# A scan chunk's 64-column products in one run with the next chunk's B and C, and the skip as diagonal products on TensorE

## The chip, the cores and the metric

The kernel runs on one core of one Trainium2 chip. The metric is the device time of an execution in microseconds; three timed runs of the kernel before gave a median of 919.21 us (915.98 to 921.51).

## What is computed

The kernel is one layer of a diffusion block over 512 latent tokens with 256 context tokens before them: a mixer (a bidirectional Mamba-2 scan beside a grouped-query attention) and a hierarchical mixture of experts. The change is in the output of the scan. For each chunk of 128 tokens, each group g of 8 heads and each of the two directions the reference computes

```python
decay = jnp.where(lower, jnp.exp(jnp.where(lower, diff, 0.0)), 0.0)
cb = jnp.einsum('bcqgn,bcsgn->bcqsg', Cc, Bc)
y_diag = jnp.einsum('bcqsgr,bcsgrp->bcqgrp', cb[..., None] * decay, xdt)
y_off = jnp.einsum('bcqgn,bcgrpn,bcqgr->bcqgrp', Cc, h_in, jnp.exp(a_cs))
...
skip = p['d_skip'].astype(F32).reshape(SSD_GROUPS, SSD_HEADS_PER_GROUP)[..., None]
y = y_f + jnp.flip(y_b, axis=1) + xs.astype(F32) * skip
```

that is, for every head the product of a 128 x 128 mixing matrix with the chunk's tokens (128 x 64), the part that comes from the carried states, and the skip: the tokens times one number for each head.

## The kernel before

The program is written for a planner: every instruction has a priority, which counts up in the order of the code unless a `with rank(p)` sets it, and the planner fixes each engine's order by priority among what it believes ready at that time. Engines then run their lists in order.

The scan is `ssd(g)` (lines 540 to 630), called for the groups 0 and 1 (lines 717 and 721). It first carries the states through the chunks (`carry`, with weighted tokens in the two buffers `wx`), and then goes over four chunks c. For each chunk:

- lines 598 to 603: the products of B and C (two halves of 64 columns, tile `CT,BT` in the trace) into the PSUM buffer `s`, copied by ScalarE to `cb`
- line 605: GpSimd multiplies the tokens with the skip (`xs`)
- lines 606 to 612: the products of C with the carried states, `of` and `ob`, and VectorE's two multiplications out of PSUM into `y` and `y2`
- `mixing` (lines 579 to 594), for each half of the heads: factors are loaded from DRAM (line 585), masked by GpSimd (line 587), taken through the exponential by ScalarE (line 590), added and multiplied with `cb` by VectorE (lines 592 and 593): the mixing matrices M of four heads
- lines 616 to 620: for each head, and for each half of 64 rows of the output, a product of M and the tokens (tile `xl,M`, 64 columns); an fp32 product is two instructions, so there are 32 for a chunk
- lines 621 to 623: GpSimd adds `xs` to `y2`, VectorE adds `y2` and the product `yd` to `y`
- for group 0, `gated` (line 632) follows

The helper `mm` (line 107) issues all products, so they have this line in the trace. Beside the scan TensorE runs the projections: for group 0 those of `in_rows(0, z_sink)` and `scan_inputs(1)` (lines 715 and 718), for group 1 those of the queries (line 728). They have 128 columns and write the tile `a`; their weights are split into two parts by ScalarE (line 75) and by VectorE or GpSimd (line 76), and `scan_inputs` has a convolution on VectorE (lines 431 and 473). Both lists start at the same priority (`scanned[0]`, `scanned[1]`), so the two kinds of products are mixed on TensorE.

Of the kernel before, what the change touches and what calls it, by code (L numbers as in the profile page):

```python
# [8 lines left out]
F32 = mybir.dt.float32  # L9
# [3 lines left out]
AF = mybir.ActivationFunctionType  # L13
OP = mybir.AluOpType
# [79 lines left out]
def hybrid_block_kernel(ctx: ExitStack, tc: tile.TileContext, I, out):  # L94
    nc = tc.nc
    PE, V, S, G, SP = nc.tensor, nc.vector, nc.scalar, nc.gpsimd, nc.sync

    def pool(name, bufs=1, side="left", space=None, stack=None):
        kw = dict(name=name, bufs=bufs, reuse_waits="tile")
        if space is not None:  # L100
            kw["space"] = space
        else:
            kw["side"] = side
        return (stack or ctx).enter_context(tc.tile_pool(**kw))

    def mm(o, a, b, first, last):
        return PE.matmul(o, lhsT=a, rhs=b, start=first, stop=last)  # L107
# [6 lines left out]
    @contextmanager  # L114
    def rank(p):

        at, tc.cur_priority = tc.cur_priority, p
        yield
        tc.cur_priority = at
# [4 lines left out]
    def brow(ap, n):  # L124
        return bass.AP(tensor=ap.tensor, offset=ap.offset, ap=[[0, 128], [1, n]])
# [8 lines left out]
    def heads(ap, n):  # L134
        return ap.rearrange("p (h d) -> p h d", h=n)
# [11 lines left out]
    def pb(tag="b", dt=F32):  # L147
        return psb.tile([128, 512], dt, name=tag, bufs=tags.get(tag, 1))
# [8 lines left out]
    ident, tri_le, tri_ge = cst[:, 0:128], cst[:, 128:256], cst[:, 256:384]  # L157
# [165 lines left out]
    dsk = sdp.tile([128, 16], F32, name="dsk")  # L323
# [90 lines left out]
    grps = {0: {}, 1: {}}  # L414
# [124 lines left out]

    def ssd(g):  # L540

        r, ys = grps[g], {}
        lb, dec, wdt, ecs = dk["lb"], dk["dec"], dk["wdt"], dk["ecs"]
        gcol = slice(g * 512, (g + 1) * 512)

        def hs(d):
            return slice(d * 16 + g * 8, d * 16 + g * 8 + 8)

        def bc8(ap):
            return ap.to_broadcast([128, 8, 64])  # L550

        def weigh(t, d):
            wx = wk.tile([128, 512], F32, name="wx")
            x = r["xc"][:, t, :] if t < 2 else r["xl"][:, t - 2, :]
            V.tensor_tensor(heads(wx, 8), heads(x, 8), bc8(wdt[:, t, hs(d), None]), op=OP.mult)
            return wx

        def carry(o, h, t, d):

            wx = weigh(t, d)  # L560
            p = pb("s")
            mm(p, r["B"][:, t, :], wx, True, True)
            V.tensor_tensor(heads(o, 8), heads(h, 8), bc8(dec[:, t, hs(d), None]), op=OP.mult)
            V.tensor_add(o, o, p)

        hb, hf = (wk.tile([128, 4, 512], F32, name=n, bufs=1) for n in ("hb", "hf"))
        for d, o in ((1, hb[:, 3, :]), (0, hf[:, 0, :])):
            p = pb("s")
            for t in range(2):
                mm(p, r["B"][:, t, :], weigh(t, d), t == 0, t == 1)  # L570
            S.activation(o, p, AF.Copy)
        for i in range(3):
            carry(hb[:, 2 - i, :], hb[:, 3 - i, :], 5 - i, 1)
            carry(hf[:, i + 1, :], hf[:, i, :], 2 + i, 0)

        ng = wk.tile([128, 512], F32, name="ng", bufs=1)
        SP.dma_start(ng, brow(I["ssd_norm_g"][gcol], 512))

        def mixing(c, hh, cb):

            bc = wk.tile([128, 2, 4, 128], F32, name="bc", bufs=BC)
            for d, sg in ((0, 1), (1, -1)):
                h0 = d * 16 + g * 8 + 4 * hh
                s = csd[c, h0:h0 + 4, :]
                SP.dma_start(bc[:, d].rearrange("p h q -> p (h q)"),
                             bass.AP(tensor=s.tensor, offset=s.offset, ap=[[0, 128], [1, 512]]))
                G.affine_select(bc[:, d], bc[:, d], pattern=[[0, 4], [sg, 128]], compare_op=OP.is_ge,  # L587
                                fill=-1e30, base=0, channel_multiplier=-sg)
                for h in range(4):
                    S.activation(bc[:, d, h, :], bc[:, d, h, :], AF.Exp, bias=lb[:, c, h0 + h:h0 + h + 1])  # L590
            M = wk.tile([128, 4, 128], F32, name="M", bufs=MB)
            V.tensor_add(M, bc[:, 0], bc[:, 1])
            V.tensor_tensor(M, M, cb[:, None, :].to_broadcast([128, 4, 128]), op=OP.mult)
            return M

        for c in range(4):
            tk_ = slice(c * 128, (c + 1) * 128)
            p = pb("s")
            for a in range(2):
                o = slice(a * 64, a * 64 + 64)  # L600
                mm(p[o, 0:128], r["BT"][:, c * 128 + a * 64:c * 128 + a * 64 + 64], r["CT"][:, tk_], True, True)
            cb = wk.tile([128, 128], F32, name="cb")
            S.activation(cb, p[:, 0:128], AF.Copy)
            xs = wk.tile([128, 512], F32, name="xs", bufs=1)
            G.tensor_tensor(heads(xs, 8), heads(r["xl"][:, c, :], 8), bc8(dsk[:, g * 8:g * 8 + 8, None]), op=OP.mult)
            of, ob = pb(), pb()
            mm(of, r["CT"][:, tk_], hf[:, c, :], True, True)
            mm(ob, r["CT"][:, tk_], hb[:, c, :], True, True)
            y = wk.tile([128, 512], F32, name="y", bufs=4)
            y2 = wk.tile([128, 512], F32, name="y2", bufs=1)  # L610
            V.tensor_tensor(heads(y, 8), heads(of, 8), bc8(ecs[:, c, hs(0), None]), op=OP.mult)
            V.tensor_tensor(heads(y2, 8), heads(ob, 8), bc8(ecs[:, c, hs(1), None]), op=OP.mult)
            yd = pb()
            for hh in range(2):
                M = mixing(c, hh, cb)
                for h in range(4):
                    hc = slice((4 * hh + h) * 64, (4 * hh + h) * 64 + 64)
                    for a in range(2):
                        o = slice(a * 64, a * 64 + 64)
                        mm(yd[o, hc], M[:, h, o], r["xl"][:, c, hc], True, True)  # L620
            G.tensor_add(y2, y2, xs)
            V.tensor_add(y, y, y2)
            V.tensor_add(y, y, yd)
            ys[c] = y
            if g == 0:
                zt = wk.tile([128, 512], F32, name="zt", bufs=1)
                SP.dma_start(zt, z_d[c * 128:(c + 1) * 128, :])
                gated(y, zt, ng)
                SP.dma_start(y_d[c * 128:(c + 1) * 128, :], y)
        return ys, ng  # L630

    def gated(y, zt, ng):
        V.scalar_tensor_tensor(y, y, 0.5, zt, op0=OP.mult, op1=OP.mult)
        ss = wk.tile([128, 1], F32, name="ss")
        S.activation(wk.tile([128, 512], F32, name="y2", bufs=1), y, AF.Square, accum_out=ss)
        V.tensor_scalar(ss, ss, 1.0 / 512, 1e-6, op0=OP.mult, op1=OP.add)
        powc(ss, ss)
        V.scalar_tensor_tensor(y, y, ss, ng, op0=OP.mult, op1=OP.mult)
# [14 lines left out]
    def gate(o, p):  # L653
        S.activation(o, p, AF.Tanh, scale=0.5)
        V.scalar_tensor_tensor(o, o, 1.0, p, op0=OP.add, op1=OP.mult)
# [58 lines left out]
    wk = pool("wk", 2, side="right", stack=ssdst)  # L714
    in_rows(0, z_sink)
    with rank(scanned[0]):
        ssd(0)
    scan_inputs(1)
    scanned[1] = tc.cur_priority
    cvst.close()  # L720
    ys, ng = ssd(1)
    tc.cur_priority = scanned[1]
    eapst = ExitStack()
# [9 lines left out]
    def last_sink(t, hb_, p):  # L733
        zt = wk.tile([128, 4, 128], F32, name="M", bufs=MB).rearrange("p h q -> p (h q)")
        gate(zt, p)
        gated(ys[t], zt, ng)
# [14 lines left out]
    wrA, ca, cb = lt("wrA", 8, 20), lt("ca", 20), lt("cb", 20)  # L751
# [923 lines left out]
```

## Time and profile before

| | us |
|---|---|
| median of three runs | 919.21 |
| lowest and highest | 915.98, 921.51 |
| the profiled execution | 912.09 |
| its span in the profile | 909.8 |
| TensorE busy | 819.1 |
| VectorE busy | 696.8 |
| ScalarE busy | 420.2 |
| GpSimd busy | 319.8 |

The profile is of one execution; its times are counted from the start of the span. A busy TensorE is not TensorE at its peak: matmuls overlap, and a matmul that waits for the array counts as busy. In the rows PE is TensorE, DVE VectorE, ACT ScalarE and POOL GpSimd; a tile is written as out<-in.

### The profile page before, as it was taken

Reading aid. Unit: us, or ns where it says so; the run is one execution under the profiler, and the core shown is the slowest. Engines: PE = TensorE matmul, PEld = TensorE weight load, DVE = VectorE, ACT = ScalarE, POOL = GpSimd, SP = SyncE. Lnnn points to the kernel's source line nnn. Section 1 sums busy time; section 2 is a strip of 40 time slices with the busy share of each in tenths; the row PEclk is TensorE's granted clock in tenths of the full one; section 3 lists DMA queues with packets and bytes.
Section 4 is the critical chain, followed back from the end, with each engine's and each line's share of the span. In section 5 each row is a group of like instructions: output and inputs, shape, how many; then the busy total and the mean of one; then the engine's idle time right before and its main releaser. Section 6 shows DMA issues by size and latency. Waiting matters only on the chain. (4 is left out here: it accounts for less than half of the span.)

```text
span 909.8 us, 13605 instructions
## 1 busy us (share of the span) xinstructions
PE 819.1 (90%) x4974; PEld 569.0 (63%) x4974; DVE 696.8 (77%) x1074; ACT 420.2 (46%) x776; POOL 319.8 (35%) x230
## 2 busy tenths in 40 slices
PE   6999998899989999999988999899982799999992
PEld 2696676556776566776655656556652577777762
DVE  3575764886967897656776787877888999899977
ACT  2253443545563144453541444444433466776652
POOL 0012211426231273410059036540314555545524
PEclk9999999999999999999997999999996799999997
DMA  9966996436343133676053011120185999999974
GB/s 300 319 195 235 286 303 215 128 116 185 104 118 83 45 118 109 202 227 170 24 151 103 13 30 62 46 83 1 53 273 207 332 350 340 331 339 343 338 212 192
DMA packets 112349, 165.54 MB, mean 182 GB/s; under 512 B 13144, under 2 KB 78200, under 8 KB 112280
## 3 DMA queue, kind: packets, MB, share of 16 engines
q1 hardware_dynamic: 105560, 141.24, 48.8%
q0 software_dynamic: 6288, 21.84, 8.4%
q10 hardware_dynamic: 432, 1.57, 0.5%
q8 instruction: 39, 0.64, 0.3%
q14 instruction: 30, 0.25, 0.1%
HBM read 142.41 MB, written 22.21 MB: 181 GB/s over the span
## 5 line engine op out<-in xcount | busy, mean ns | idle before, releaser
L75 ACT ACTIVATE whi<-wraw 128x1024 fp32r<-128x1024 f32 (+1 forms) x100 | 104.1, 1045 | 74.7 <-PE a L107 40.8
L76 DVE TENSOR_TENSOR wlo<-wraw,whi 128x1024 fp32r<-128x1024 f32 (+1 forms) x73 | 94.7, 1303 | 24.0 <-ACT whi L75 23.3
L967 ACT ACTIVATE hxh<-b 128x512 f32<-128x512 f32 x96 | 55.7, 595 | 88.9 <-PE b L107 88.2
L76 POOL TENSOR_TENSOR wlo<-wraw,whi 128x1024 fp32r<-128x1024 f32 (+1 forms) x22 | 53.5, 2432 | 117.9 <-ACT whi L75 98.5
L943 DVE TENSOR_REDUCE mx<-s 128x1 f32<-128x768 f32 x64 | 61.0, 953 | 34.3 <-PE s L107 34.2
L473 DVE SCALAR_TENSOR_TENSOR acc<-u,cols,acc 128x770 f32<-128x770 f32 (+1 forms) x48 | 56.8, 1182 | 28.5 <-ACT acc L465 23.0
L107 PE MATMUL a<-whi,hxh 128*128 128x512 f32 (+2 forms) x176 | 70.7, 403 | 1.8 <-ACT hxh L263 1.8
L107 PE MATMUL a<-wlo,hxh 128*128 128x512 f32 (+2 forms) x176 | 69.8, 397 | 0.2 <-DVE wlo L76 0.2
L107 PE MATMUL a<-whi,hxl 128*128 128x512 f32 (+2 forms) x176 | 69.1, 394 | 0.0
L107 PE MATMUL a<-hxl,whi 128*128 128x512 f32 (+1 forms) x176 | 64.5, 367 | 0.0
L107 PE MATMUL a<-hxh,whi 128*128 128x512 f32 (+1 forms) x176 | 64.1, 364 | 0.0
L107 PE MATMUL a<-hxh,wlo 128*128 128x512 f32 (+1 forms) x176 | 63.9, 363 | 0.0
L590 ACT ACTIVATE bc<-bc,lb 128x128 f32<-128x128 f32 x128 | 40.6, 392 | 13.5 <-POOL bc L587 13.3
L107 PE MATMUL a<-whi,xh 128*128 128x512 f32 x102 | 43.8, 429 | 0.0
L1435 POOL DMA_INDIRECT acc<-y,rowi x15 | 26.5, 1768 | 48.5 <-DVE wlo L76 29.6
L107 PE MATMUL a<-wlo,xh 128*128 128x512 f32 x102 | 41.1, 402 | 0.1
L107 PE MATMUL a<-whi,xl 128*128 128x512 f32 x102 | 40.9, 401 | 0.0
L107 PEld LDWEIGHTS a<-whi,hxh 128*128 128x128 f32 x176 | 33.9, 193 | 10.9 <-issue 4.2
L107 PEld LDWEIGHTS a<-wlo,hxh 128*128 128x128 f32 x176 | 34.0, 193 | 9.7 <-issue 4.9
L107 PEld LDWEIGHTS a<-hxh,wlo 128*128 128x128 f32 x176 | 33.9, 193 | 9.2 <-issue 5.3
L107 PEld LDWEIGHTS a<-whi,hxl 128*128 128x128 f32 x176 | 33.7, 192 | 9.3 <-issue 4.6
L107 PEld LDWEIGHTS a<-hxl,whi 128*128 128x128 f32 x176 | 34.0, 193 | 7.4 <-issue 3.6
(489 smaller groups left out, 2169.4 us busy)
## 6 DMA issues: line engine op xcount, KB each, us to landing
wraw<-in_w_mod_dram SPq DMA_DIRECT2D x32, 512.0 KB
wraw<-in_w_in_dram SPq DMA_DIRECT2D x30, 512.0 KB
wraw<-in_w_down_dram SPq DMA_DIRECT2D x22, 512.0 KB
wraw<-in_w_gate_dram SPq DMA_DIRECT2D x40, 256.0 KB
wraw<-in_w_up_dram SPq DMA_DIRECT2D x40, 256.0 KB
mraw<-in_w_mod_dram SPq DMA_DIRECT2D x32, 256.0 KB
bc<-csd SPq DMA_DIRECT2D x32, 256.0 KB
wraw<-in_w_out_dram SPq DMA_DIRECT2D x8, 512.0 KB
```

The costliest lines, as they stand in the source:

```text
L75: self.nc.scalar.activation(hi, raw, AF.Copy)
L76: self.lo_engine(i).tensor_sub(lo, raw, hi.bitcast(F32))
L107: return PE.matmul(o, lhsT=a, rhs=b, start=first, stop=last)
L473: V.scalar_tensor_tensor(a, uk, wk_, a, op0=OP.mult, op1=OP.add)
L590: S.activation(bc[:, d, h, :], bc[:, d, h, :], AF.Exp, bias=lb[:, c, h0 + h:h0 + h + 1])
L943: V.tensor_reduce(mx[u][:, g:g + 1], pss_[:, 768 * i:768 * i + 768], axis=AX, op=OP.max)
L967: S.activation(PT[u][:, k], p, AF.Exp)
L1435: G.indirect_dma_start(out=acc, out_offset=bass.IndirectOffsetOnAxis(ap=rows, axis=0), in_=y, in_offset=None, compute_op=OP.add)
```

## The change

The skip becomes a product: for each head ScalarE makes a diagonal matrix (the identity times the head's number), kept in the two buffers `wx`, and TensorE adds the diagonal's product with the tokens to the product with M, in the same PSUM accumulation. GpSimd's multiplication and addition go. All products of a chunk are issued after both Ms are made, from the last head to the first, and are ranked at the priority that the scan began with; the products of B and C of the next chunk follow them there, so that they are no longer at the head of the chunk's loop.

```diff
--- before.py
+++ after.py
@@ -539,7 +539,7 @@
 
     def ssd(g):
 
-        r, ys = grps[g], {}
+        r, ys, first = grps[g], {}, tc.cur_priority
         lb, dec, wdt, ecs = dk["lb"], dk["dec"], dk["wdt"], dk["ecs"]
         gcol = slice(g * 512, (g + 1) * 512)
 
@@ -593,16 +593,22 @@
             V.tensor_tensor(M, M, cb[:, None, :].to_broadcast([128, 4, 128]), op=OP.mult)
             return M
 
-        for c in range(4):
-            tk_ = slice(c * 128, (c + 1) * 128)
+        def pairs(c):
+
             p = pb("s")
             for a in range(2):
                 o = slice(a * 64, a * 64 + 64)
-                mm(p[o, 0:128], r["BT"][:, c * 128 + a * 64:c * 128 + a * 64 + 64], r["CT"][:, tk_], True, True)
+                mm(p[o, 0:128], r["BT"][:, c * 128 + a * 64:c * 128 + a * 64 + 64], r["CT"][:, c * 128:c * 128 + 128], True, True)
+            return p[:, 0:128]
+
+        skip = [wk.tile([128, 4, 128], F32, name="wx") for _ in range(2)]
+        for h in range(8):
+            S.activation(skip[h // 4][:, h % 4], ident, AF.Copy, scale=dsk[:, g * 8 + h:g * 8 + h + 1])
+        p = pairs(0)
+        for c in range(4):
+            tk_ = slice(c * 128, (c + 1) * 128)
             cb = wk.tile([128, 128], F32, name="cb")
-            S.activation(cb, p[:, 0:128], AF.Copy)
-            xs = wk.tile([128, 512], F32, name="xs", bufs=1)
-            G.tensor_tensor(heads(xs, 8), heads(r["xl"][:, c, :], 8), bc8(dsk[:, g * 8:g * 8 + 8, None]), op=OP.mult)
+            S.activation(cb, p, AF.Copy)
             of, ob = pb(), pb()
             mm(of, r["CT"][:, tk_], hf[:, c, :], True, True)
             mm(ob, r["CT"][:, tk_], hb[:, c, :], True, True)
@@ -610,15 +616,17 @@
             y2 = wk.tile([128, 512], F32, name="y2", bufs=1)
             V.tensor_tensor(heads(y, 8), heads(of, 8), bc8(ecs[:, c, hs(0), None]), op=OP.mult)
             V.tensor_tensor(heads(y2, 8), heads(ob, 8), bc8(ecs[:, c, hs(1), None]), op=OP.mult)
-            yd = pb()
-            for hh in range(2):
-                M = mixing(c, hh, cb)
-                for h in range(4):
-                    hc = slice((4 * hh + h) * 64, (4 * hh + h) * 64 + 64)
+            yd, Ms = pb(), [mixing(c, hh, cb) for hh in range(2)]
+
+            with rank(first):
+                for h in reversed(range(8)):
+                    hc = slice(h * 64, h * 64 + 64)
                     for a in range(2):
                         o = slice(a * 64, a * 64 + 64)
-                        mm(yd[o, hc], M[:, h, o], r["xl"][:, c, hc], True, True)
-            G.tensor_add(y2, y2, xs)
+                        mm(yd[o, hc], Ms[h // 4][:, h % 4, o], r["xl"][:, c, hc], True, False)
+                        mm(yd[o, hc], skip[h // 4][:, h % 4, o], r["xl"][:, c, hc], False, True)
+                if c < 3:
+                    p = pairs(c + 1)
             V.tensor_add(y, y, y2)
             V.tensor_add(y, y, yd)
             ys[c] = y
```

## Rows read from the trace of the kernel before

**Rows 1.** Busy time by stretch: length, PE, PEld, DVE, ACT, POOL, clock, DMA, GB/s

```profile
186.00:220.00 34.00, 32.83 (x166) 20.90 (x165) 23.43 (x30) 13.71 (x38) 15.02 (x16) 1.00 0.61 166
220.00:258.00 38.00, 34.86 (x209) 25.36 (x207) 35.16 (x40) 22.75 (x57) 17.82 (x18) 1.00 0.45 131
```

**Rows 2.** Timeline of PE, short 64-column runs: start, length, instructions

```profile
195.03 0.33 PE L107 MATMUL b<-xl,M 128*64 128x64 f32 x2
204.58 0.34 PE L107 MATMUL b<-xl,M 128*64 128x64 f32 x4
...
356.52 0.33 PE L107 MATMUL b<-xl,M 128*64 128x64 f32 x2
357.21 0.33 PE L107 MATMUL b<-xl,M 128*64 128x64 f32 x2
```

**Rows 3.** Timeline of PE around the scan's last run of 16

```profile
361.01 0.39 PE L107 MATMUL a<-whi,hxl 128*128 128x512 f32 x1
361.33 0.69 PE L107 MATMUL b<-xl,M 128*64 128x64 f32 x16
361.95 0.50 PE L107 MATMUL a<-whi,hxh 128*128 128x512 f32 x1
362.28 0.39 PE L107 MATMUL a<-wlo,hxh 128*128 128x512 f32 x1
362.51 0.40 PE L107 MATMUL a<-whi,hxl 128*128 128x512 f32 x1
```

**Rows 4.** Timeline of PE, products of B and C standing alone

```profile
189.88 0.44 PE L107 MATMUL s<-CT,BT 128*64 128x128 f32 x4
199.19 0.43 PE L107 MATMUL s<-CT,BT 128*64 128x128 f32 x2
...
199.98 0.43 PE L107 MATMUL s<-CT,BT 128*64 128x128 f32 x2
...
345.05 0.43 PE L107 MATMUL s<-CT,BT 128*64 128x128 f32 x2
```

**Rows 5.** Timeline of PE, a run with B and C behind it

```profile
323.63 0.69 PE L107 MATMUL b<-xl,M 128*64 128x64 f32 x16
324.14 0.39 PE L107 MATMUL s<-CT,BT 128*64 128x128 f32 x4
324.46 0.50 PE L107 MATMUL a<-whi,hxh 128*128 128x512 f32 x1
```

**Rows 6.** PE's waits from 186 to 366 us: in total, times, longest

```profile
PE t L443 <- DVE acc L431: 6.2, 2, 4.1
PE b L107 <- DVE M L593: 5.7, 7, 1.9
```

**Rows 7.** Timeline of PE around the longest wait for M

```profile
330.96 0.69 PE L107 MATMUL b<-xl,M 128*64 128x64 f32 x16 [1.92 <-DVE M L593]
...
332.56 0.63 PE L107 MATMUL a<-whi,hxh 128*128 128x512 f32 x1
```

**Rows 8.** Tile M on DVE (least, median, most ns), and a timeline at 309.7 us

```profile
L593 DVE TENSOR_TENSOR M<-M,cb x16: 677/804/1780, 190.7 to 351.9; 128x512 f32<-128x512 f32 x16
...
309.72 1.29 POOL L621 TENSOR_TENSOR y<-y,xs 128x512 f32<-128x512 f32 x1 [17.03 <-DVE y L612]
309.81 3.19 DVE L593 TENSOR_TENSOR M<-M,cb 128x512 f32<-128x512 f32 x2 [0.23 <-ACT cb L603]
```

**Rows 9.** Groups of POOL by line, 160 to 366 us: busy us, mean ns, idle before

```profile
L621 POOL TENSOR_TENSOR y<-y,xs 128x512 f32<-128x512 f32 x8 | 12.9, 1612 | 27.6 <-DVE y L612 27.5
L605 POOL TENSOR_TENSOR xs<-xl,dsk 128x512 f32<-128x512 f32 x8 | 11.5, 1432 | 6.6 <-ACT xl L447 6.2
```

**Rows 10.** Timeline of ACT, the copies of B and C in each first chunk

```profile
190.37 0.28 ACT L603 ACTIVATE cb<-s 128x128 f32<-128x128 f32 x1 [5.38 <-PE s L107]
...
309.50 0.28 ACT L603 ACTIVATE cb<-s 128x128 f32<-128x128 f32 x1 [8.03 <-PE s L107]
```

**Rows 11.** Groups of ACT by line, 160 to 366 us: busy us, mean ns, idle before

```profile
L590 ACT ACTIVATE bc<-bc,lb 128x128 f32<-128x128 f32 x128 | 40.6, 392 | 13.5 <-POOL bc L587 13.3
```

## The prediction

> **What bounds the kernel now.** I read the busy table by stretch first. While the scan runs, TensorE has work for 32.8 of 34.0 us in 186 to 220 us and for 34.9 of 38.0 us in 220 to 258 us, at the full clock; VectorE has 23.4 and then 35.2 us [rows 1]. So in the first stretch TensorE alone sets the pace, and in the second VectorE is as full. What is to be seen is that the scan's small products do not stand alone: the projections (tiles `a`) run on the same engine between them.
>
> The TensorE timeline shows what one such interruption costs. A projection matmul follows the last one every 0.23 us when nothing comes between (362.28 to 362.51) [rows 3]. Around a pair of 64-column products the step from one pair to the next, with one projection matmul in between, is 0.69 us (356.52 to 357.21) [rows 2], so the pair costs 0.69 - 0.23 = 0.46 us, although four such instructions take only 0.01 us longer than two (0.34 against 0.33) [rows 2]. The price is in the switch between 128 and 64 columns, not in the products. A run of 16 costs 361.01 to 362.28, 1.27 us, less two projection steps of 0.23: 0.81 us [rows 3]. From 4 to 16 instructions the run grows from 0.34 to 0.69 us: 29 ns for each [rows 2, 3].
>
> The waits come next: TensorE stood 5.7 us in seven waits for the mixing matrix M, and 6.2 us in two for the convolution on VectorE [rows 6]. After the longest wait for M (1.92 us) projection matmuls took 0.63 us [rows 7] where 0.39 to 0.40 is normal [rows 3]: the 1.2 GHz level, and eight of them stepped by some 0.43 instead of 0.23 us, about 1.6 us more.
>
> **The change part by part.** *Fewer runs, removed.* Following all 64-column products of both groups in the timeline I count 59 runs. 36 are short ones of M's products (first at 195.03, last at 357.21) [rows 2]: 36 x 0.46 = 16.6 us. 11 are of B and C alone (first at 189.88, last at 345.05), 199.98 - 199.19 - 0.23 = 0.56 us each: 6.2 us [rows 4]. Two of eight instructions lie between the short and the long price, 0.58 each: 1.2 us. Ten have 16 or more, 323.63, 330.96 and 361.33 among them, 0.81 each: 8.1 us [rows 3, 5, 7]. B and C joined to a run cost 0.83 (323.63 to 324.46) less 0.62 (361.33 to 361.95), 0.21 us [rows 3, 5]; that happened about one and a half times: 0.3 us. Sum before: 32.4 us.
>
> *One run for each chunk, with the diagonal products, added.* Each fp32 product is two instructions, so a chunk has 32 with M and now 32 with the diagonal: 64. A run of 64 costs 0.81 + 48 x 0.029 = 2.2 us; eight make 17.6 us, 7.4 us of it the 256 added instructions. The products of B and C cost 0.21 in the same run (six times, the first of each group alone at 0.56: together 2.4 us) or 0.56 each alone (4.5 us). I take alone: they need only the buffer `s`, free as soon as `cb` is copied, and in the trace of before they went ahead of products with M that were earlier in the code but not ready [rows 5, 7]. Sum after: 22.1 us, or 20.0 if joined. TensorE saves 10.3 us, up to 12.4.
>
> *Order of the halves, not shown before.* Now four instructions for one half of the columns follow each other before four for the other half come; before it was two and two. The two halves ran side by side: two more instructions, in the other half, added 0.01 us [rows 2]. With both halves side by side each steps by 2 x 29 = 58 ns. If the instructions started strictly in the code's order, four of a half would hold up the other half: eight would take 6 x 58 = 348 ns, 43.5 each instead of 29, or 14.5 ns x 64 x 8 = 7.4 us more. Below, the bound is zero. I take zero, because the rows show the other half's first starting ahead of the same half's second. The Trainium skill (TensorE: Matmul & The Clock Gate, The mechanism) states that matmuls start and end in strict program order, without reordering. By that rule the 7.4 us would be paid; the trace does not agree with it for two column halves, as the 0.01 us shows.
>
> *GpSimd's two steps, removed.* They were 12.9 and 11.5 us of GpSimd [rows 9]. VectorE waited little for them, but shared with them: M times `cb` takes 0.68 at best and up to 1.78 us [rows 8], and beside the addition at 309.72 two of them took 3.19 us, 1.8 too long, just before the products that TensorE waited for [rows 8]. So the VectorE chain to M gets shorter, by 0 to 1.8 us at such a place. Behind the addition on GpSimd stood the selects that build M's factors and the weight splits; these can now go earlier. On SP nothing is added or moved.
>
> *The diagonals on ScalarE, added.* 16 copies of 128x128. A copy of this size took 0.28 us out of PSUM [rows 10], one with an exponential 0.39 us [rows 11]: 4.5 to 6.3 us in all. ScalarE was idle 5.4 and 8.0 us just before `cb` of the two first chunks [rows 10], so I cost them at nothing; uncovered they would hold `cb`, the exponentials and the splits behind them for up to 3.1 us in each group, as they reuse the `wx` buffers and can only start when the last state products have read these.
>
> *A new wait.* The run begins with the heads of the second M, so all products now wait for both Ms, and what waits behind them on TensorE are the projections, for which ScalarE's copies and splits wait in turn. Being ranked first, the run is placed at the first moment at which the planner believes M ready. Before, seven waits cost 5.7 us [rows 6]; eight runs may wait between 0 and 1.9 us each. Against the old waits and the slow clock (7.3 us) I take 6.3: a gain of 2 us for the shorter chain, a loss of 1 for both Ms and the diagonals.
>
> **Sum.** -10.3 on TensorE, -1.0 on waits, +2.3 because in 220 to 258 us VectorE is nearly as full as TensorE [rows 1] and part of the gain turns into waits for the convolution: -9.0 us. The profiled execution took 912.1 us (its span 909.8 and 2.3 around it), so 903.1; the runs' median of 919.2 lies 0.8% higher, and the same 9 us there give 910.2, call it 910.
>
> **Rivals.** *More than the sum* (chance 0.13). The runs join, the 7.3 us of waits and slow clock go, and VectorE keeps up: -12.4 - 7.3 = about -19, 900 us. For it: GpSimd lay in M's chain. Against: the projections' own chain on VectorE stays.
>
> *VectorE takes it back* (0.12). Only the first stretch, where TensorE alone is full, gains: its two chunks have 23 runs of 11.4 us by the prices above, against 5.5 after, so 5.9 us less; the six others turn theirs into waits for VectorE, and waiting for both Ms costs some 2 us: about -4, 915 us, within what counts as no change. For it: 35.2 of 38.0 us [rows 1].
>
> *Strict order, so the change does not do what it says* (0.10). The 7.4 us above are paid: -9.0 + 7.4 = -1.6, 917.6 us. Against it: [rows 2].
>
> *Slower* (0.13). Each of the eight ranked runs waits for M as long as the longest did, 1.92 us, and pays 1.6 us of slow clock behind it [rows 7]: 8 x 3.5 = 28 us in place of 7.3, less the 10.3 saved: +10, 930 us. It decides when a run loses more than (10.3 + 7.3) / 8 = 2.2 us on average. For it: the run can no longer begin with the first M, and nothing may overtake it on TensorE. Against: the first M's products waited as well, and the chain to M loses GpSimd.
>
> **How the numbers follow.** The forecast (gain of 5 to 14 us) has 0.52. About 0.5% is what a measurement can tell from no change here, 4.6 us. Faster: forecast, the larger gain and a little of the second rival, 0.66. Within: 0.22. Slower: 0.12. The range goes from 899 (the full gain with all waits gone) to 921, which covers strict order and VectorE, and leaves out most of the slower case.
>
> **What would show it.** The page of after should have 256 more TensorE matmuls, and GpSimd some 24 us less busy. The timeline should show eight runs of 64 in 2.0 to 2.2 us from the first product to the next projection; 2.8 or more means strict order. B and C standing alone before the run shows that they did not join. M times `cb` should stay near 0.7 us. TensorE's waits for M above 10 us in sum would mean the slower case; waits for the convolution above 10 us would mean that VectorE took the gain back. If the end of the scan (the last run, at 361.33 before) comes 9 us earlier and the total doesn't, the step that failed is that the later stages simply follow.

## The result, and the profile after

The changed kernel takes 908.59 us (905.33 to 910.15, four runs) against 920.22 us of the kernel before, run beside it: a ratio of 0.9877, 95% interval 0.9834 to 0.992. Run twice more, on two chips, it gave 0.9905 (0.9867 to 0.9943) and 0.9880 (0.9847 to 0.9912). That is 9 to 11 us, where the prediction had 9. The profiled execution took 908.13 us (before 912.09). The three profiled executions of the changed kernel had spans from 902.6 to 909.4 us, so totals are compared by the timed runs below, and profiles only tell where the time lies.

The page's busy times of the changed kernel, by engine, with the number of instructions:

```profile
PE 807.6 (89%) x5230; PEld 570.3 (63%) x5230; DVE 681.6 (75%) x1074; ACT 424.5 (47%) x792; POOL 297.6 (33%) x214
```

TensorE has its 256 added instructions (5230 for 4974) and is still 11.5 us less busy. GpSimd lost 22 us. The reading that the prediction did not have is VectorE: the same 1074 instructions, 15 us less busy.

The stretches of [rows 1] in the changed kernel, and the whole scan from 186 to 362 us (columns as in [rows 1]):

```profile
186.00:220.00 34.00, 29.76 (x298) 21.26 (x297) 24.26 (x38) 17.64 (x52) 9.58 (x13) 1.00 0.65 190
220.00:258.00 38.00, 32.84 (x220) 27.09 (x219) 31.06 (x36) 27.81 (x69) 14.05 (x16) 0.96 0.48 129
186.00:362.00 176.00, 160.82 (x1157) 121.22 (x1156) 134.63 (x194) 87.60 (x204) 53.00 (x45) 0.98 0.41 119
```

And the whole scan in the kernel before:

```profile
186.00:362.00 176.00, 164.17 (x866) 114.11 (x864) 141.19 (x181) 79.29 (x185) 68.77 (x58) 0.98 0.39 113
```

In the same 176 us VectorE now does more instructions (194 for 181) in 6.6 us less, and TensorE has 4.2 us unused in the first stretch where it had 1.2. TensorE's 64-column products stand in 14 runs in place of 59. One of them in the TensorE timeline, its first and last instructions and the projections around it:

```profile
340.10 0.39 PE L107 MATMUL a<-whi,hxl 128*128 128x512 f32 x1
340.42 0.34 PE L107 MATMUL b<-xl,M 128*64 128x64 f32 x4
340.58 0.29 PE L107 MATMUL b<-xl,wx 128*64 128x64 f32 x4
340.70 0.33 PE L107 MATMUL b<-xl,M 128*64 128x64 f32 x4
...
342.21 0.34 PE L107 MATMUL b<-xl,wx 128*64 128x64 f32 x4
342.48 0.50 PE L107 MATMUL a<-whi,hxh 128*128 128x512 f32 x1
342.81 0.39 PE L107 MATMUL a<-wlo,hxh 128*128 128x512 f32 x1
```

From 340.10 to 342.81, less two projection steps of 0.23, the run of 64 costs 2.25 us. Four instructions follow the last four every 0.117 us, 29 ns each. In the code two instructions with M and two with the diagonal follow each other for one half of the columns; the timeline has four with M and then four with the diagonal, so the two halves start side by side. Six of the eight products of B and C stand alone, three at each group's start, and two joined the first run of a group:

```profile
189.63 0.44 PE L107 MATMUL s<-CT,BT 128*64 128x128 f32 x4
190.00 0.50 PE L107 MATMUL a<-whi,hxl 128*128 128x512 f32 x1
190.34 0.40 PE L107 MATMUL a<-whi,hxh 128*128 128x512 f32 x1
190.66 0.44 PE L107 MATMUL s<-CT,BT 128*64 128x128 f32 x4
```

(190.66 - 189.63 - 2 x 0.23 = 0.57 us each.) What TensorE waits for from 186 to 366 us, against [rows 6]:

```profile
PE b L107 <- DVE y L617: 6.7, 4, 2.6
PE t L443 <- DVE acc L431: 5.3, 3, 2.7
PE b L107 <- DVE y L631: 1.9, 1, 1.9
PE b L107 <- DVE y L618: 1.3, 1, 1.3
```

The waits for M (5.7 us) are gone, and 9.9 us of waits for one of the two buffers `b` stand in their place (8.0 and 7.9 us in the two other profiles): VectorE has not yet read the products of C with the states, or `yd`. The scan's end is where ScalarE reads the last result of the projections beside it, before and after:

```profile
361.44 0.60 ACT L666 ACTIVATE qx<-a 128x512 f32<-128x512 f32 x1 [0.76 <-PE a L107]
```

```profile
353.70 0.60 ACT L674 ACTIVATE qx<-a 128x512 f32<-128x512 f32 x1 [0.59 <-PE a L107]
```

7.7 us earlier in this pair; 7.5 and 11.7 us earlier (353.9 and 349.8) in the two other profiles of the changed kernel. From there to the end of the span the profile of before took 548.4 us and the three of the changed kernel 552.6 to 555.5, so in the profiles only 0.4 to 7.2 us of the gain are left at the end. There is one profile of before, of an execution 7 us below the median of 919.21; whether the stages after the scan lose something stays open.

### The profile page after: what moved, and what is told of

Its sections match the earlier page's. It is cut to its first block, busy times and chain, and to the rows that moved or that the text cites. A ratio compares the mean times of both kernels' runs of the same rounds, so it can differ in the third digit from the quotient of the medians.

```text
span 906.3 us, 14112 instructions
## 1 busy us (share of the span) xinstructions
PE 807.6 (89%) x5230; PEld 570.3 (63%) x5230; DVE 681.6 (75%) x1074; ACT 424.5 (47%) x792; POOL 297.6 (33%) x214
## 5 line engine op out<-in xcount | busy, mean ns | idle before, releaser
L76 DVE TENSOR_TENSOR wlo<-wraw,whi 128x1024 fp32r<-128x1024 f32 (+1 forms) x73 | 93.7, 1289 | 29.6 <-ACT whi L75 28.9
L107 PE MATMUL a<-wlo,hxh 128*128 128x512 f32 (+2 forms) x176 | 69.6, 396 | 0.2 <-DVE wlo L76 0.2
L107 PE MATMUL a<-hxl,whi 128*128 128x512 f32 (+1 forms) x176 | 62.4, 355 | 0.0
L107 PE MATMUL a<-hxh,wlo 128*128 128x512 f32 (+1 forms) x176 | 61.9, 351 | 0.0
L587 POOL TENSOR_SCALAR_AFFINE_SELECT bc<-bc 128x512 f32<-128x512 f32 x32 | 27.7, 874 | 52.5 <-DMA bc<-csd 49.7
```

What stands on the lines that cost most here:

```text
L76: self.lo_engine(i).tensor_sub(lo, raw, hi.bitcast(F32))
```

## The experiments

Twelve runs in three groups; a group shared one chip and its runs of the kernel before. Microseconds are worked out from the ratio on record and that chip's median of the kernel before (916.87, 918.74 and 918.77). The medians alone give other values: -5.7 us for e5, -10.5 and -13.0 for e3, -6.9 and -10.7 for the changed kernel, 26.3 for e2 and 24.7 for e4. A difference of two rows is good to some 5 us.

| kernel | runs of 64 columns | skip | ratio (95%) | us |
|---|---|---|---|---|
| before | 59 | GpSimd | 1 | 0 |
| e1 runs only | 14 | GpSimd | 1.0015 (0.9978 to 1.0053) | +1.4 |
| e5 old order, no skip | 59 | none | 0.9922 (0.9894 to 0.9949) | -7.2 |
| e3 no skip | 14 | none | 0.9852 (0.9811 to 0.9893), again 0.9839 (0.9801 to 0.9878) | -13.6, -14.8 |
| e7 dead steps | 14 | GpSimd, unused | 0.9977 (0.9948 to 1.0006), again 0.9964 (0.9937 to 0.9991) | -2.1, -3.3 |
| changed kernel | 14 | diagonals | 0.9905, again 0.9880 | -8.7, -11.0 |
| e6 other buffers | 10 | diagonals | 0.9961 (0.9933 to 0.9989), again 0.9945 (0.9912 to 0.9977) | -3.6, -5.1 |
| e2 diagonals only | 124 | diagonals | 1.0322 (1.0257 to 1.0387) | +29.6 |
| e4 no rank | 136 | diagonals | 1.0326 (1.0259 to 1.0393) | +30.0 |

**First group: the two halves of the change.** e1 keeps the changed order and leaves the skip on GpSimd:

```diff
+            xs = wk.tile([128, 512], F32, name="xs", bufs=1)
+            G.tensor_tensor(heads(xs, 8), heads(r["xl"][:, c, :], 8), bc8(dsk[...]), op=OP.mult)
...
-                        mm(yd[o, hc], skip[h // 4][:, h % 4, o], r["xl"][:, c, hc], False, True)
...
+            G.tensor_add(y2, y2, xs)
```

> The chunk's products are made and ranked as in the changed kernel (14 runs of 64-column products), but without the diagonals: the skip stays GpSimd's multiplication and addition. If the number of runs makes the time (my theory): the 256 added instructions are gone, 256 x 0.030 = 7.7 us of TensorE, so some 903 us, 3 to 8 below the changed kernel (908.6), unless GpSimd's steps take it back. If the gain came from taking the skip off GpSimd (the rival): within 4 us of the kernel before, 916 to 920.

e3 is the changed kernel without the diagonals and without any skip (the skip is missing from its output):

```diff
-        skip = [wk.tile([128, 4, 128], F32, name="wx") for _ in range(2)]
...
-                        mm(yd[o, hc], skip[h // 4][:, h % 4, o], r["xl"][:, c, hc], False, True)
```

> The changed kernel without the diagonals and without any skip (the skip is left out of the output, 14 runs). My theory: what the 256 added instructions cost when TensorE is the bound, 256 x 0.030 = 7.7 us below the changed kernel, some 901 us. Rival (TensorE is not the bound in the scan once the runs are long; the buffers and VectorE are): no more than 2 us below it. Against the run with the skip on GpSimd it shows what GpSimd's two steps cost: 0 to 3 us by my theory, 8 or more by the rival that GpSimd made the gain.

e5 is the kernel before without its skip (missing from its output too):

```diff
-            xs = wk.tile([128, 512], F32, name="xs", bufs=1)
-            G.tensor_tensor(heads(xs, 8), heads(r["xl"][:, c, :], 8), bc8(dsk[...]), op=OP.mult)
...
-            G.tensor_add(y2, y2, xs)
```

> The kernel before with its order of products kept (59 runs) and the skip left out of the output: GpSimd's multiplication and addition are gone and nothing replaces them. My theory: the relief of VectorE alone, 0 to 4 us below the kernel before, 916 to 920. Rival (the gain is GpSimd's): the whole gain of the change or more, 908 or less.

The changed kernel itself ran beside them.

> The changed kernel once more beside the others, to have its ratio more narrowly: 0.9877 with an interval of 0.983 to 0.992 was measured; 0.985 to 0.991 expected.

Measured: e1 gains nothing. In its profile what TensorE saves is lost again, in waits that are twice those of [rows 6]:

```profile
PE b L107 <- DVE M L593: 8.2, 4, 4.0
PE t L443 <- DVE acc L431: 7.8, 3, 4.2
PE b L107 <- DVE y L617: 4.7, 1, 4.7
PE b L107 <- DVE y L630: 2.4, 2, 1.8
PE b L107 <- DVE y L616: 1.4, 1, 1.4
```

24.5 us, against 11.9 before. The whole scan of e1 (columns as in [rows 1]) shows what follows: TensorE has work for 151.28 of 176 us (before 164.17) and its mean clock falls from 0.98 to 0.93.

```profile
186.00:362.00 176.00, 151.28 (x863) 110.36 (x862) 135.36 (x176) 78.70 (x183) 65.21 (x57) 0.93 0.41 113
```

After its longest wait the run of 32 itself took 1.98 us, at a granted clock of 0.50 (the 1.2 GHz level), where others of e1 took 1.15:

```profile
338.40 1.98 PE L107 MATMUL b<-xl,M 128*64 128x64 f32 x32 [4.02 <-DVE M L593]
```

So the theory that the number of runs makes the time, by which e1 would have taken some 903 us, failed; GpSimd's steps cost more than the 0 to 4 us that it gave them.

The four kernels make a square. GpSimd's two steps cost 7.2 us in the old order (before to e5) and 15.0 us in the new one (e1 to e3); by medians 5.7 and 11.7. Fewer runs are worth -1.4 us while GpSimd has the skip (before to e1) and 6.4 us without it (e5 to e3); by medians -1.2 and 4.8. So fewer runs show no value of their own, and GpSimd's removal is worth some twice as much with them, 7.8 us more by the ratios with an uncertainty of some 6. The reading is that what one engine saves, the one that is next in line takes, until that is relieved too. From e3 to the changed kernel the diagonals cost 4.9 us (3.6 by medians).

**Second group: the price of a run, the buffers, and what of GpSimd costs.** e2 has the order of before and the diagonals:

```diff
+        skip = [wk.tile([128, 4, 128], F32, name="wx") for _ in range(2)]
+        for h in range(8):
+            S.activation(skip[h // 4][:, h % 4], ident, AF.Copy, scale=dsk[...])
...
-                        mm(yd[o, hc], M[:, h, o], r["xl"][:, c, hc], True, True)
-            G.tensor_add(y2, y2, xs)
+                        mm(yd[o, hc], M[:, h, o], r["xl"][:, c, hc], True, False)
+                        mm(yd[o, hc], skip[hh][:, h, o], r["xl"][:, c, hc], False, True)
```

> The order of the kernel before, with one edit: the diagonal products take the place of GpSimd's two steps. The placement that results has 124 runs of 64-column products, 65 more than before. If a run's price is the switch (0.46 us for each short one), TensorE gets about 30 us more work and GpSimd's part gives back the 5.7 us of the kernel that leaves the skip out in the old order: about 24 us slower than before, ratio 1.02 to 1.03. If instead GpSimd's steps were all that the change gained from and the number of runs hardly counts, this kernel has the same gain as the changed one or a little less: ratio 0.99 to 1.00.

e4 is the changed kernel with the products left to the planner:

```diff
-            with rank(first):
+            with ExitStack():
```

> The changed kernel with the ranking of the products taken away, so that the planner spreads them: 136 runs of 64-column products in place of 14, the same instructions otherwise. By the price of a switch (0.3 to 0.46 us for each of 122 more runs) 37 to 56 us of TensorE's time are lost, and what TensorE waits for M would be less than before: 25 to 50 us slower than the changed kernel, ratio 1.015 to 1.045 against the kernel before. If runs hardly count while VectorE sets the pace, it stays within 5 us of the changed kernel: ratio 0.99 to 1.00.

Measured: +29.6 and +30.0 us, e2 a little above its 1.02 to 1.03 and e4 as expected. The TensorE timeline of e2 has the pattern of [rows 2], now with M and diagonal in turn:

```profile
196.19 0.33 PE L107 MATMUL b<-xl,M 128*64 128x64 f32 x2
196.45 0.50 PE L107 MATMUL a<-whi,hxh 128*128 128x512 f32 x1
196.88 0.33 PE L107 MATMUL b<-xl,wx 128*64 128x64 f32 x2
197.14 0.51 PE L107 MATMUL a<-wlo,hxh 128*128 128x512 f32 x1
197.57 0.33 PE L107 MATMUL b<-xl,M 128*64 128x64 f32 x2
```

0.69 us from run to run, so 0.46 each, as before. From e5 to e2 the time rises by 36.8 us (29.6 + 7.2, the two on different chips); by medians 32.0. The estimate from the prices: a run costs 0.46 us with up to four instructions, and 29 ns for each further one. The 124 runs of e2 come to 64.6 us and the 59 of e5 to 31.3, so 33.3 more. The price of a switch is borne out, and so is that it is paid in full where TensorE sets the pace: in e2 TensorE has work for

```profile
186.00:362.00 176.00, 172.19 (x968) 116.05 (x966) 117.79 (x161) 79.91 (x193) 48.09 (x42) 0.99 0.39 106
```

172.2 of the 176 us, and VectorE only 117.8. From the changed kernel to e4 it is 39 to 41 us for 122 more runs (32 to 35 by medians). By the same prices the 136 runs of e4 come to 69.6 us and the 14 of the changed kernel to 20.6, so 49.0 more; TensorE's waits fell by 10.8 us meanwhile (15.2 in the changed kernel, 4.4 in e4), which leaves 38. (122 x 0.46 would be 56, but counts the time of the products twice, as both kernels have the same ones.)

e6 tries the waits for the buffers `b`: all four chunks' B and C go to one buffer `s` at the group's start, `yd` goes to a buffer `s`.

```diff
-        p = pairs(0)
+        p, cbs = pb("s"), wk.tile([128, 4, 128], F32, name="cb", bufs=1)
+        for c in range(4):
+            pairs(c)
+        S.activation(cbs, p.rearrange("p (c q) -> p c q", c=4), AF.Copy)
...
-            yd, Ms = pb(), [mixing(c, hh, cb) for hh in range(2)]
+            yd, Ms = pb("s"), [mixing(c, hh, cb) for hh in range(2)]
```

> The changed kernel, with the products of B and C of all four chunks made at the start of a group into one buffer s and copied once, and the products with M written to a buffer s instead of b, so that the two buffers b only serve the two products with the states. In the changed kernel TensorE stood 9.9 us in waits for VectorE to read a buffer b. If these waits set the time, they go and 3 to 6 us are gained against the changed kernel (ratio against the kernel before 0.981 to 0.987). If VectorE's own chain sets it, the waits move to the convolution's products or to M and nothing is gained (0.987 to 0.992).

Its waits of TensorE in the scan:

```profile
PE t L443 <- DVE acc L431: 6.9, 3, 3.7
PE s L107 <- DVE y L629: 5.6, 4, 2.3
PE s L107 <- DVE M L593: 4.4, 2, 3.2
PE b L107 <- DVE y L618: 0.5, 1, 0.5
PE b L107 <- DVE y L617: 0.2, 1, 0.2
```

The waits for `b` went from 9.9 to 0.7 us, and as much came back as waits for VectorE to read `yd` and to make M. Nothing is gained: the buffers only say at which place TensorE meets VectorE. (e6 also makes all four chunks' B and C at once, which no run separates.)

e7 is e3 with GpSimd's two steps put back as dead work: same size, same places, the result read by nobody (the skip is missing from its output).

```diff
+            xs = wk.tile([128, 512], F32, name="xs", bufs=1)
+            G.tensor_tensor(heads(xs, 8), heads(r["xl"][:, c, :], 8), bc8(dsk[...]), op=OP.mult)
...
+            G.tensor_add(xs, xs, y2)
             V.tensor_add(y, y, y2)
```

> The changed kernel's order without the diagonals, and with both GpSimd steps still run at their places and in their size, but into a tile that nobody reads, so that the skip is missing from the output. VectorE no longer waits for GpSimd's addition before its own. If VectorE's wait in order was what the steps cost (11.6 us between the kernel with one run and GpSimd's skip, 1.0015, and the one without the skip, 0.985), this kernel is near the latter: ratio 0.985 to 0.990. If it is GpSimd's sharing with VectorE, or its own queue with the selects behind the steps, it is near the former: 0.997 to 1.003. Between the two, both have a part.

Measured 0.9977, near e1 and far from e3: most of the cost is there although VectorE waits for no result of these steps. But it ran on another chip than e3, and the profiled spans were only 3.8 us apart. So e3, e7, e6 and the changed kernel ran once more together.

**Third group: the same on one chip.**

> The changed kernel with the skip left out altogether, once more, beside the kernel with GpSimd's dead steps on one chip: the two were run on different chips, and their ratios to the kernel before (0.985 and 0.998) are 12 us apart while their profiled spans are 3.8 us apart (906.8 and 910.6). If GpSimd's work alone, by sharing and in its queue, costs most of the 12 us, this kernel is again 8 us or more faster than the one with the dead steps. If the distance came from the chips, it is 3 to 5 us.

> The same kernel as the one with GpSimd's dead steps (the skip missing from the output), once more. If sharing and GpSimd's queue carry most of what the steps cost, it is 8 us or more slower than the kernel without the skip on the same chip (ratio about 0.995 to 1.000); if VectorE's wait in order carries most of it, 3 to 5 us slower (0.989 to 0.994).

> The kernel with B and C made in one buffer and the products with M in a buffer s, once more, beside the changed kernel on one chip. Its scan ended with the changed kernel's (last read of the projections' result at 353.7 us in both), so on one chip the two should be within 2 us of each other; if the change itself loses something, it is again 5 to 7 us slower.

> The changed kernel itself, as the measure for the other three on this chip: 0.988 to 0.991 of the kernel before, as in the two measurements so far (0.9877 and 0.9905). By the theory that the diagonals cost some 3.6 us, the kernel without the skip is that much faster.

Measured: 905.73 us for e3, 914.95 for e7, 912.66 for e6 and 908.06 for the changed kernel. The dead steps cost 11.5 us by the ratios (0.9839 and 0.9964), 9.2 by the medians, as expected if their work alone carries most of it; of the 15.0 us from e1 to e3 (11.7 by medians) that leaves 2 to 5 us for VectorE's wait in order, across chips. In e1's profile these waits are 2.4 us. The diagonals cost 3.8 us (2.3 by medians). e6 is 4.6 us slower than the changed kernel (6.0 by the ratios), against the expected 2 at most, so it loses something. In its first profile the scan ended with the changed kernel's (353.7), in its second 7 us later; what it loses is open.

How dead work of GpSimd costs time is to be seen at one place. The same two instructions of VectorE, M times `cb` of the second group's first chunk, in e3 and in e7, and GpSimd's steps in e7:

```profile
302.72 1.29 DVE L593 TENSOR_TENSOR M<-M,cb 128x512 f32<-128x512 f32 x2 [0.23 <-ACT cb L608]
```

```profile
304.13 3.19 DVE L593 TENSOR_TENSOR M<-M,cb 128x512 f32<-128x512 f32 x2 [0.23 <-ACT cb L608]
...
304.04 1.28 POOL L628 TENSOR_TENSOR xs<-xs,y 128x512 f32<-128x512 f32 x1 [17.28 <-DVE y L617]
305.40 1.37 POOL L610 TENSOR_TENSOR xs<-xl,dsk 128x512 f32<-128x512 f32 x1
```

GpSimd had nothing at this place in e3. Over the scan, VectorE's groups (busy us, mean ns) of M times `cb`, M's addition and `y` plus `y2` read in e7 (second profile)

```profile
L593 DVE TENSOR_TENSOR M<-M,cb 128x512 f32<-128x512 f32 x16 | 16.7, 1059 | 0.3 <-ACT cb L608 0.2
L592 DVE TENSOR_TENSOR M<-bc 128x512 f32<-128x512 f32 x14 | 11.2, 802 | 1.4 <-ACT bc L590 1.4
L629 DVE TENSOR_TENSOR y<-y,y 128x512 f32<-128x512 f32 x8 | 8.0, 996 | 0.1
L617 DVE TENSOR_TENSOR y<-b,ecs 128x512 f32<-128x512 f32 x8 | 5.5, 683 | 1.1 <-PE b L107 1.1
```

and in e3 (second profile)

```profile
L593 DVE TENSOR_TENSOR M<-M,cb 128x512 f32<-128x512 f32 x16 | 14.5, 923 | 0.2 <-ACT cb L608 0.2
L592 DVE TENSOR_TENSOR M<-bc 128x512 f32<-128x512 f32 x14 | 10.5, 754 | 2.8 <-PE b L107 2.2 <-ACT bc L590 0.6
L626 DVE TENSOR_TENSOR y<-y,y 128x512 f32<-128x512 f32 x8 | 5.9, 738 | 0.0
L615 DVE TENSOR_TENSOR y<-b,ecs 128x512 f32<-128x512 f32 x8 | 5.4, 680 | 0.2 <-PE b L107 0.2
```

The first three groups are 35.9 us against 30.9: 5.0 us longer for 21.6 us of GpSimd's dead work. The fourth, which takes one of its inputs from PSUM, is unmoved. In the whole scan VectorE is 6.0 us busier (5.1 in the first pair of profiles), and the scan ends 5.2 us later (355.30 against 350.13; 4.0 in the first pair). So VectorE's chain accounts for about half of the 9 to 11 us; the rest lies in what single profiles cannot place (e3's profiled execution was above its median, e7's below). The rival of GpSimd's queue, where the selects stand behind the dead steps, shows little here: VectorE's waits for the exponentials behind these selects (`bc`) are 1.4 us in e7 against 0.6 in e3, and 1.4 against 1.9 in the first pair.

## Why the prediction was right in its number and half wrong in its working

**What bounds the kernel: half right.** TensorE has the work, but in the scan it was level with VectorE's chain of M and `y` in more places than [rows 1] showed. e1 tells it: with TensorE's part reduced and VectorE's not, the time stays. The busy share of VectorE (23.4 of 34.0 us) hid this, because a chain that is late does not need a full engine.

**Fewer runs: price right, worth wrong.** The run of 64 cost 2.25 us (2.2 predicted), B and C alone 0.57 (0.56), and after the change the sum is 8 x 2.25 + 6 x 0.57 + 2 x 0.21 = 21.8 us (22.1 predicted). e2 confirms the 0.46 us of a switch. But of the 10.3 us only a part came: 6.4 us from e5 to e3, less 3.8 to 4.9 us for the diagonals, so 1.5 to 2.6 us net, with an uncertainty larger than that, and none with GpSimd's steps in place. B and C: six of the eight stayed alone as assumed, but three at each group's start instead of one before each run; two joined the first run of their group.

**Order of the halves: right.** 29 ns for each of 64 instructions, no sign of 43.5. The rival of strict order would have given runs of 3.1 us. That one half's first instruction starts ahead of the other half's second could not be read from [rows 2], which merge the instructions; the changed kernel's timeline shows it.

**GpSimd's steps: the term that was mis-sized.** "VectorE waited little for them" was true and beside the point. The prediction saw the 3.19 us at 309.81 [rows 8] and priced it as 0 to 1.8 us "at such a place", inside a net -1.0 us for all waits. Measured it is -7.2 us in the old order and -15.0 in the new one (-5.7 and -11.7 by medians), most of it without any wait for a result (9.2 to 11.5 us from e7 to e3). What the prediction should have summed is all VectorE instructions that stand beside GpSimd's 24.4 us: over the whole kernel VectorE's busy time fell by 15 us with the same instructions, and by 6.9 and 10.8 us from e7 to e3, where only GpSimd's dead work goes.

**Diagonals on ScalarE: right.** They took 387 ns each, 16 in all, and no instruction waits for them in the trace. What diagonals cost (3.8 to 4.9 us, 2.3 to 3.6 by medians) is below the 7.4 us of TensorE that the prediction had put inside the run.

**The new wait: not as large as the "slower" rival had it, and why is only in part shown.** In the changed kernel no wait of TensorE is put down to M. In e1 8.2 us are, the longest 4.0, with the slow clock behind: the mechanism of that rival. But e3, without GpSimd's steps, also has 5.7 and 4.5 us of waits for M (longest 3.7) in its two profiles, and is the fastest kernel of all; so GpSimd's removal alone does not take these waits away. **Taking back by VectorE** was put at 2.3 us as waits for the convolution, a size for which the prediction gives no working; these waits fell (6.2 to 5.3), and it came as 7.9 to 9.9 us of waits for the buffers `b`. In sum TensorE waits 15.2 us where it waited 11.9, 3.3 us more, where the prediction had 1.3 more with the slow clock included.

So -10.3 and -1.0 were the wrong shares of a right sum, and that the sum came out is luck: two thirds to four fifths of the gain (7.2 of 9 to 11 us) come with GpSimd's removal alone, the rest from the runs, and the second is only to be had with the first. The end of the scan came 7.5 to 11.7 us earlier (9 predicted), and the timed runs 9 to 11; that the later stages simply followed is not shown by the profiles, as said above.

## What to carry to other kernels

Price an edit on each engine of a chain, and then ask which engine stands next: here 12.9 us less work in the scan on the engine that is fullest (e1) was worth nothing until the engine that feeds it was relieved, and some 5 to 6 us afterwards. Work on GpSimd is not free because GpSimd is idle: count the VectorE instructions beside it that read two operands from SBUF. And when columns change between products, count the switches (0.46 us for a run of two to four instructions here) before the products (29 ns for each further instruction).

## What the runs showed of the hardware

Where VectorE multiplies M with `cb` while a GpSimd split (`wlo`) is already running, it ends at a fixed distance behind GpSimd's instruction. In the changed kernel and at two places of e3 (second profile):

```profile
309.05 2.81 POOL L76 TENSOR_TENSOR wlo<-wraw,whi 128x1024 fp32r<-128x1024 f32 x1 [29.51 <-ACT whi L75]
309.68 2.72 DVE L593 TENSOR_TENSOR M<-M,cb 128x512 f32<-128x512 f32 x1
```

```profile
306.31 2.36 POOL L76 TENSOR_TENSOR wlo<-wraw,whi 128x1024 fp32r<-128x1024 f32 x1 [29.54 <-ACT whi L75]
306.96 2.26 DVE L593 TENSOR_TENSOR M<-M,cb 128x512 f32<-128x512 f32 x1
...
335.24 2.55 POOL L76 TENSOR_TENSOR wlo<-wraw,whi 128x1024 fp32r<-128x1024 f32 x1 [2.35 <-ACT whi L75]
335.50 2.84 DVE L593 TENSOR_TENSOR M<-M,cb 128x512 f32<-128x512 f32 x1
```

GpSimd ends at 311.86, 308.67 and 337.79, VectorE at 312.40, 309.22 and 338.34: 0.54, 0.55 and 0.55 us later, though VectorE started up to 2.3 us before that end and needs 0.68 us alone. The dead steps of e7 did the same above: the second ends at 306.77, VectorE's pair at 307.32. So VectorE did not run slower beside GpSimd; it stood until GpSimd was done. It goes the other way too. Where a select of GpSimd starts during VectorE's instruction, the select ends 0.49 us behind it and takes 1.13 us, where the next one takes 0.64 (the changed kernel):

```profile
218.81 0.69 DVE L593 TENSOR_TENSOR M<-M,cb 128x512 f32<-128x512 f32 x1
218.86 1.13 POOL L587 TENSOR_SCALAR_AFFINE_SELECT bc<-bc 128x512 f32<-128x512 f32 x1 [1.36 <-DMA bc<-csd]
```

The Trainium skill (SBUF — State Buffer, SBUF: two separate sides) says this: an instruction of VectorE with two inputs in SBUF and one of GpSimd that reads SBUF hold a shared pair of ports in turn, the one that starts first for its whole instruction. The trace agrees, also in that VectorE's multiplications out of PSUM (`y` from `b`, 675 to 692 ns in the changed kernel) were never held up. Not every instruction of GpSimd holds VectorE, though: beside one of only 128x8 elements (L132, 324.88 to 327.69 us in e3's second profile) M times `cb` took 0.67 us. GpSimd's splits still stand in VectorE's way in the changed kernel; moving them was not tried.
